# One wide product for both parts of the moving operand in the paired up-projection of a two-layer decoder

## The chip, the cores and the metric

The kernel runs on one core of a Trainium2 chip. The metric is the device time of one execution in microseconds, shown as the median of the runs. The profiled execution is a run of its own; its span (first to last instruction) is a little shorter than its time.

## The reference, cut to what matters

Two layers over 512 tokens of width 1024. Each layer has a mixing half (attention and retention from one joint projection, then gates and an output projection) and an MLP. The change is in the MLP alone:

```python
    h2 = rmsnorm(x, g_mlp)
    x = x + jnp.square(jax.nn.relu(h2 @ w_up)) @ w_down      # w_up 1024 x 4096, w_down 4096 x 1024
```

## The kernel before, in words

**Precision.** Everything is float32, but TensorE gets float32r, which keeps fewer bits. So each operand is split into a high part (a rounded copy, written by ACT) and a low part (the rest, a subtraction on DVE). A product of two such operands is three products of TensorE: high by high, high by low, low by high. The helper `products` (L276) issues them at L282, L283 and L284: weights `ah`/`al`, moving operand `bh`/`bl`.

**Weights.** They stream in 1024-column units (`raw`), in the fixed order of `unit_order`. `unit` (L243) hands out the next unit and has `split_until` (L218) split the units up to two ahead: high part on ACT (L237), low part on DVE (L238), into tiles `hi` and `lo` of a pool of three. Within these tiles the weights may begin `ASIDE` = 48 elements (192 bytes) in. With it their address lies 192 bytes from that of the moving operand, counted modulo 512; without it the distance is none.

**The MLP.** Hidden rows come in chunks of 128. The first four chunks are plain products of 512 columns (`group`). The other 28 pairs of chunks (14 a layer) use a scheme of Winograd's kind: w_up's contraction of 1024 is cut in two halves, the 512 tokens in two halves of H = 256, and a pair of chunks is computed with seven half products in place of eight. The price is sums and differences: of the moving operand once a layer (`sum_input`, L981, eight forms in tiles `by_form`), and of the weights for each pair (`add_part`, L204: L208, L211, L215, L216 on DVE). One half product is a call of `multiply` in `pair` (L1025): four k-steps, each three products of 256 columns. `block` (L1002) gives the k-steps of the input itself (tiles `xh`, `xl`), `form` (L999) those of the sums.

In `pair`, three PSUM banks (the first 256 columns of each) collect the results, in this order of the source:

```text
a  = block(0,0)              L1039  ACT copies a into b
e  = form(0)                 L1041  ACT copies e to eu
b += form(1)                 L1044  ACT copies b to eu
a += block(1,0)              L1046  DVE: z from a, relu and rstd
b += form(2)                 L1049  DVE: z from b + eu
e += block(1,1)              L1051  DVE: z from e + eu
b += form(3)                 L1055  DVE: relu and rstd of two quarters
                             L1056  DVE: z from b, relu and rstd
```

Then ACT squares z (L1059), and z is split into high and low (`split`: L289 on ACT, L290 on DVE) for w_down. w_down's products run in `two_chunks` (L344), with 512 columns, 48 for two output chunks; L1066 adds them to x. `mlp_sequence` alternates: two pairs first, then two chunks of w_down with the hidden rows of one quarter, then a pair of the next quarter, and so on. At the end of each quarter w_down needs the pair just made.

**Order.** The source's order is not the order of the queues: the framework's scheduler places each engine's instructions when the program is built, and takes w_down's products in between where a pair's operands are not ready by its reckoning. In the queue of TensorE, form(3) of a regular pair follows some 22 products of w_down. Each engine works its own queue in order and waits on semaphores. The DMAs of weights are issued on SP.

Of the kernel before, what the change touches and what calls it, by code (L numbers as in the profile page):

```python
# [11 lines left out]
F32R = mybir.dt.float32r  # L12
AF = mybir.ActivationFunctionType
# [102 lines left out]
def decoder(ctx, tc, xT, x_first, w_in, w_a, w_b, w_out, w_up, w_down, tables, decay, band, out):  # L116
# [29 lines left out]
    sink = little_x[:, P - n_gain - n_sink : P - n_gain]  # L146
    eps, half, nsink = (little_x[:, a : a + n] for a, n in ((0, 1), (8, N_KV), (16, n_sink)))
    x = little_x[:, P:].rearrange("p (k t) -> p k t", t=T)
    xh = const.tile([P, KD, T], F32R, name="xh")
    xl = const.tile([P, KD, T], F32R, name="xl")  # L150
    slots = Slots([const.tile([P, 4, T], F32R, name=f"r{i}") for i in range(9)])
    spill = dram.tile([P, KD, T], F32, name="spill")

# [64 lines left out]
    def split_until(n):  # L218
        while state["split"] < min(n, len(order)):
            i = state["split"]  # L220
            load_until(i + 3)
            paired = order[i][1] == "pair"
            if paired:
                add_part(i)
            raw = raws[i]
            if homes and i >= len(order) - len(homes):
                home = homes[len(order) - 1 - i]
                hi, lo = (home[:, 2 * a : 2 * a + 2, :].rearrange("p a t -> p (a t)") for a in range(2))
            else:

                first = ASIDE if paired or i >= len(order) - 8 else 0
                hi, lo = (wpool.tile([P, UNIT + P], F32R, tag=n, name=n)[:, first : first + UNIT] for n in ("hi", "lo"))
            for at in (LEFT,) if paired and order[i][3] == 3 else halves(i):
                if i == 0 and at.start == 0:
                    nc.vector.tensor_copy(hi[:, at], raw[:, at])
                else:
                    nc.scalar.activation(hi[:, at], raw[:, at], AF.Copy)  # L237
                nc.vector.tensor_tensor(lo[:, at], raw[:, at], f32(hi[:, at]), ALU.subtract)  # L238
            raws.pop(i - 3 if paired else i, None)
            parts[i] = (hi, lo)  # L240
            state["split"] += 1
# [240 lines left out]
    def layer_body(layer):  # L482
# [493 lines left out]

        H = T // 2
        sums = [slots.four() for _ in range(4)]
        by_form = [t[0].rearrange("p a (b t) -> p (a b) t", t=H) for t in sums]

        def sum_input(ks):  # L981

            b = [big("xg") for _ in range(2)]
            for i in range(2):
                for part, g in ((0, ks + i), (1, ks + i + 4)):
                    col = g_mlp * KD + g
                    nc.scalar.activation(b[part][:, i, :], x[:, g, :], AF.Copy, scale=gain[:, col : col + 1])
# [3 lines left out]
            hi, lo = by_form[ks // 2], by_form[2 + ks // 2]  # L991
            nc.vector.tensor_tensor(t1, b12, b11, ALU.subtract)
            nc.vector.tensor_tensor(t2, b22, t1, ALU.subtract)
            split(hi[:, 0:4, :], lo[:, 0:4, :], f[0])
            nc.vector.tensor_tensor(t3, b22, b12, ALU.subtract)
            nc.vector.tensor_tensor(t4, b21, t2, ALU.subtract)
            split(hi[:, 4:8, :], lo[:, 4:8, :], f[1])

        def form(j):  # L999
            return [tuple(by_form[2 * i + k // 2][:, 2 * j + k % 2, :] for i in range(2)) for k in range(4)]  # L1000

        def block(half, tokens):  # L1002
            at = slice(tokens * H, tokens * H + H)
            return [(xh[:, k, at], xl[:, k, at]) for k in range(4 * half, 4 * half + 4)]

        up = [[] for _ in range(4)]
        up_slots = [[] for _ in range(4)]
# [16 lines left out]

        def pair(q):  # L1025
            def multiply(ps, weights, left, moving, start=True):
                hi, lo = weights
                cols = [slice((0 if left else 4 * P) + k * P, (0 if left else 4 * P) + (k + 1) * P) for k in range(4)]
                products(ps, [((hi[:, c], lo[:, c]), m) for c, m in zip(cols, moving)], start, True, not start)

            a, e, b = (bank(ps_mm, "mm")[:, :H] for _ in range(3))
            eu, z = temp("eu"), big("z")
            part = unit("pair", layer)
            multiply(a, part, True, block(0, 0))
            nc.scalar.activation(b, a, AF.Copy)  # L1039
            multiply(e, part, False, form(0))  # L1040
            nc.scalar.activation(eu[:, :H], e, AF.Copy)  # L1041
            part = unit("pair", layer)
            multiply(b, part, True, form(1), False)
            nc.scalar.activation(eu[:, H:], b, AF.Copy)  # L1044
            multiply(a, part, False, block(1, 0), False)
            nc.vector.scalar_tensor_tensor(z[:, 0, :H], a, 0.0, rms_mlp.value[:, :H], ALU.max, ALU.mult)  # L1046
            part = unit("pair", layer)
            multiply(b, part, True, form(2), False)
            nc.vector.tensor_tensor(z[:, 1, H:], b, eu[:, :H], ALU.add)  # L1049
            multiply(e, part, False, block(1, 1), False)  # L1050
            nc.vector.tensor_tensor(z[:, 0, H:], e, eu[:, H:], ALU.add)  # L1051
# [204 lines left out]
```

## Time and profile before

| | |
|---|---|
| Median of 3 runs (lowest to highest) | 1505.5 us (1505.16 to 1505.73) |
| Profiled execution: time, span | 1504.93 us, 1503.1 us |
| Granted clock of TensorE in it | 0.998 |
| DMA, mean | 103 GB/s |
| Starts of L1039, five regular pairs | 487.1, 507.9, 528.7, 548.1, 570.2 us |
| L237, split of 1024 on ACT, mean of one | 1058 ns |
| L238, split of 1024 on DVE, mean of one | 1221 ns |

An instruction's mean duration is not what it costs its engine: products overlap on TensorE. In the lists, "idle before" is idle time of the engine just before the instructions of a group, with what ended most of it.

### The profile page before, as it was taken

How to read it: one execution, taken by the hardware profiler on the slowest of the kernel's cores; microseconds unless marked ns; L12 is line 12 of the kernel's file. 1: busy time of each engine (PE TensorE's matmuls, PEld its weight loads, DVE VectorE, ACT ScalarE, POOL GpSimd, SP SyncE). 2: the span in 40 equal slices, each digit the busy share in tenths (PEclk: the TensorE clock that was granted, in tenths of full speed). 3: DMA queues.
4: the chain of work that ended last, by engine and by line, in shares of the span. 5: the costliest groups of instructions: out<-in, count | busy, mean ns of one | idle time of the engine just before them, and what ended most of it. 6: DMA issues, size and time to landing. Idle time of an engine off the chain costs nothing.

```text
span 1503.1 us, 20508 instructions
## 1 busy us (share of the span) xinstructions
PE 1491.8 (99%) x8082; PEld 1296.0 (86%) x8082; DVE 1026.7 (68%) x1598; ACT 738.8 (49%) x1163; POOL 2.9 (0%) x13
## 2 busy tenths in 40 slices
PE   9999999999999999999999999999999999999997
PEld 7888888888888999989888888888888999899997
DVE  7877568754787666676678865777449866666664
ACT  6657355532564444444455742555326544444452
POOL 0000000000000000000000000000000000000000
PEclk9999999999999999999999999999999999999999
DMA  6422222234223233233442222222342232232331
GB/s 221 133 85 71 98 84 92 70 126 126 99 75 108 99 113 99 98 100 124 160 130 92 85 85 98 80 83 84 127 126 96 87 99 99 99 112 99 102 109 56
DMA packets 52640, 155.10 MB, mean 103 GB/s; under 512 B 6208, under 2 KB 8384, under 8 KB 52544
## 3 DMA queue, kind: packets, MB, share of 16 engines
q1 hardware_dynamic: 52400, 153.54, 31.1%
q8 instruction: 63, 1.03, 0.3%
q14 instruction: 33, 0.27, 0.1%
q10 hardware_dynamic: 144, 0.26, 0.1%
HBM read 146.96 MB, written 4.19 MB: 101 GB/s over the span
## 4 chain that ended last, share of the span: by engine, by line
PE 99%; ACT 1%; DVE 0%; issue 0%; DVEq 0%
PE mm L284 29%; PE mm L282 29%; PE mm L283 29%; PE rv L282 2%; PE rv L284 2%; PE rv L283 2%; PE score L653 1%; PE pT L618 1%; PE r L284 1%; PE r L283 1%; PE r L282 1%; PE pv L638 0%; PE pv L639 0%; PE ssq L376 0%; PE ret L283 0%; PE ret L284 0%
## 5 line engine op out<-in xcount | busy, mean ns | idle before, releaser
L237 ACT ACTIVATE hi<-raw 128x1024 fp32r<-128x1024 f32 (+1 forms) x313 | 314.7, 1013 | 504.0 <-PE mm L283 413.8
L238 DVE TENSOR_TENSOR lo<-raw,hi 128x1024 fp32r<-128x1024 f32 (+1 forms) x314 | 362.4, 1163 | 157.1 <-ACT hi L237 156.3
L283 PE MATMUL mm<-r,hi 128*128 128x512 f32 (+1 forms) x1136 | 390.2, 344 | 0.0
L282 PE MATMUL mm<-r,hi 128*128 128x512 f32 (+1 forms) x1136 | 387.7, 345 | 1.1 <-ACT mm L1039 1.1
L284 PE MATMUL mm<-r,lo 128*128 128x512 f32 (+1 forms) x1136 | 386.6, 344 | 0.0
L282 PE MATMUL mm<-xh,hi 128*128 128x512 f32 (+1 forms) x1008 | 356.4, 355 | 0.0
L283 PE MATMUL mm<-xl,hi 128*128 128x512 f32 (+1 forms) x1008 | 355.4, 354 | 0.0
L284 PE MATMUL mm<-xh,lo 128*128 128x512 f32 (+1 forms) x1008 | 354.7, 354 | 0.0
L282 PEld LDWEIGHTS mm<-r,hi 128*128 128x128 f32 x1136 | 212.5, 187 | 27.5 <-ACT mm L1039 1.5
L283 PEld LDWEIGHTS mm<-r,hi 128*128 128x128 f32 x1136 | 213.3, 188 | 26.0
L284 PEld LDWEIGHTS mm<-r,lo 128*128 128x128 f32 x1136 | 213.1, 188 | 25.6
L283 PEld LDWEIGHTS mm<-xl,hi 128*128 128x128 f32 x1008 | 189.5, 188 | 25.3
L282 PEld LDWEIGHTS mm<-xh,hi 128*128 128x128 f32 x1008 | 189.1, 188 | 25.7 <-ACT xh L292 0.5
L284 PEld LDWEIGHTS mm<-xh,lo 128*128 128x128 f32 x1008 | 189.3, 188 | 25.1
L1066 DVE TENSOR_TENSOR x<-x,mm 128x512 f32<-128x512 f32 x56 | 37.8, 686 | 33.7 <-PE mm L284 33.7
L284 PE MATMUL rv<-hi,xl 128*128 128x512 f32 x128 | 49.8, 389 | 0.0
L283 PE MATMUL rv<-lo,xh 128*128 128x512 f32 x128 | 49.8, 389 | 0.0
L282 PE MATMUL rv<-hi,xh 128*128 128x512 f32 x128 | 49.8, 390 | 0.0
L283 PE MATMUL mm<-ulo,hi 128*128 128x512 f32 (+1 forms) x128 | 46.1, 362 | 0.0
L282 PE MATMUL mm<-uhi,hi 128*128 128x512 f32 (+1 forms) x128 | 46.1, 362 | 0.0
L284 PE MATMUL mm<-uhi,lo 128*128 128x512 f32 (+1 forms) x128 | 45.5, 363 | 0.0
L1046 DVE SCALAR_TENSOR_TENSOR z<-mm,rstd 128x256 f32<-128x256 f32 x28 | 11.9, 425 | 40.2 <-PE mm L284 40.2
(188 smaller groups left out, 1683.3 us busy)
## 6 DMA issues: line engine op xcount, KB each, us to landing
raw<-w_in_in SPq DMA_DIRECT2D x89, 512.0 KB, 3.4
raw<-w_down_in SPq DMA_DIRECT2D x64, 512.0 KB, 3.3
raw<-w_up_in SPq DMA_DIRECT2D x36, 512.0 KB, 3.3
raw<-w_up_in SPq DMA_DIRECT2D x56, 256.0 KB, 2.7
raw<-w_b_in SPq DMA_DIRECT2D x16, 512.0 KB, 3.3
raw<-w_out_in SPq DMA_DIRECT2D x16, 512.0 KB, 4.0
raw<-w_a_in SPq DMA_DIRECT2D x8, 512.0 KB, 3.3
x<-xT_in SPq DMA_DIRECT2D x15, 256.0 KB, 3.8
```

What stands on the lines that cost most here:

```text
L237: nc.scalar.activation(hi[:, at], raw[:, at], AF.Copy)
L238: nc.vector.tensor_tensor(lo[:, at], raw[:, at], f32(hi[:, at]), ALU.subtract)
L282: nc.tensor.matmul(ps, ah, bh, start=start and i == 0, stop=False, **more)
L283: nc.tensor.matmul(ps, ah, bl, start=False, stop=False, **more)
L284: nc.tensor.matmul(ps, al, bh, start=False, stop=stop and i == n - 1, **more)
L618: nc.tensor.transpose(pt[:, i * P : (i + 1) * P], sm[:, at : at + P], ident)
L653: nc.tensor.matmul(ps[:, g * w : (g + 1) * w], q_s[g][:, c, at], part[:, keys], start=i == 0, stop=i == 1)
L1046: nc.vector.scalar_tensor_tensor(z[:, 0, :H], a, 0.0, rms_mlp.value[:, :H], ALU.max, ALU.mult)
L1066: nc.vector.tensor_tensor(x[:, c, :], x[:, c, :], ps, ALU.add)
```

## The change

High weights now meet both parts of the moving operand in one product. The moving operand is laid out so that its high and low parts of 256 columns can be given as one operand of 512: `xh` and `xl` become two halves of one tile `xhl`, and the sums' forms are stored with the two parts of each form side by side. The product writes a whole bank: high by high in the left half, high by low in the right half. The low weights meet the high part alone and add to the left half. So a k-step is a product of 512 and one of 256 in place of three of 256, and the halves of a bank must be added when it is read: by `join` (a copy of the right half on ACT, an add on DVE) or, where a copied bank is added as well, by `join_copied` (three adds on DVE). The copies of banks are of 512 columns. The weights of the pairs begin at 0 in their tiles in place of `ASIDE`. Relu and rstd of the first token half are taken together, like those of the second.

```diff
-    xh = const.tile([P, KD, T], F32R, name="xh")
-    xl = const.tile([P, KD, T], F32R, name="xl")
+    xhl = const.tile([P, 2, KD, T], F32R, name="xhl")
+    xh, xl = xhl[:, 0], xhl[:, 1]
...
-                first = ASIDE if paired or i >= len(order) - 8 else 0
-                hi, lo = (wpool.tile([P, UNIT + P], F32R, tag=n, name=n)[:, first : first + UNIT] for n in ("hi", "lo"))
+                first = (0, 0) if paired else (ASIDE, ASIDE) if i >= len(order) - 8 else (0, 0)
+                hi, lo = (
+                    wpool.tile([P, UNIT + P], F32R, tag=n, name=n)[:, a : a + UNIT] for n, a in zip(("hi", "lo"), first)
+                )
...
-        by_form = [t[0].rearrange("p a (b t) -> p (a b) t", t=H) for t in sums]
+        by_form = [
+            t[0].rearrange("p a (b t) -> p (a b) t", t=H).rearrange("p (j k s) t -> p j k s t", k=2, s=2) for t in sums
+        ]
...
-            split(hi[:, 0:4, :], lo[:, 0:4, :], f[0])
+            split(*parts_of_forms(ks, 0), f[0].rearrange("p (j k) t -> p j k t", k=2))
...
-            return [tuple(by_form[2 * i + k // 2][:, 2 * j + k % 2, :] for i in range(2)) for k in range(4)]
+            return [by_form[2 * (j // 2) + k // 2][:, j % 2, k % 2, :, :] for k in range(4)]
...
-            return [(xh[:, k, at], xl[:, k, at]) for k in range(4 * half, 4 * half + 4)]
+            return [xhl[:, :, k, at] for k in range(4 * half, 4 * half + 4)]
...
                 hi, lo = weights
-                cols = [slice((0 if left else 4 * P) + k * P, (0 if left else 4 * P) + (k + 1) * P) for k in range(4)]
-                products(ps, [((hi[:, c], lo[:, c]), m) for c, m in zip(cols, moving)], start, True, not start)
-            a, e, b = (bank(ps_mm, "mm")[:, :H] for _ in range(3))
-            eu, z = temp("eu"), big("z")
+                more = {} if start else {"skip_group_check": True}
+                both = ps.rearrange("p (s t) -> p s t", t=H)
+                for k, m in enumerate(moving):
+                    c = slice((0 if left else 4 * P) + k * P, (0 if left else 4 * P) + (k + 1) * P)
+                    nc.tensor.matmul(both, hi[:, c], m, start=start and k == 0, stop=False, **more)
+                    nc.tensor.matmul(ps[:, :H], lo[:, c], m[:, 0, :], start=False, stop=k == 3 and start, **more)
+
+            def join(dest, ps):
+                side = temp("side")[:, :H]
+                nc.scalar.activation(side, ps[:, H:], AF.Copy)
+                nc.vector.tensor_tensor(dest, ps[:, :H], side, ALU.add)
+
+            def join_copied(dest, ps, u):
+                nc.vector.tensor_tensor(u[:, :H], u[:, :H], u[:, H:], ALU.add)
+                nc.vector.tensor_tensor(u[:, :H], u[:, :H], ps[:, H:], ALU.add)
+                nc.vector.tensor_tensor(dest, ps[:, :H], u[:, :H], ALU.add)
+
+            a, e, b = (bank(ps_mm, "mm") for _ in range(3))
+            eu, bu, z = temp("eu"), temp("bu"), big("z")
...
-            nc.scalar.activation(eu[:, :H], e, AF.Copy)
+            nc.scalar.activation(eu, e, AF.Copy)
...
-            nc.scalar.activation(eu[:, H:], b, AF.Copy)
+            nc.scalar.activation(bu, b, AF.Copy)
             multiply(a, part, False, block(1, 0), False)
-            nc.vector.scalar_tensor_tensor(z[:, 0, :H], a, 0.0, rms_mlp.value[:, :H], ALU.max, ALU.mult)
+            join(z[:, 0, :H], a)
...
-            nc.vector.tensor_tensor(z[:, 1, H:], b, eu[:, :H], ALU.add)
+            join_copied(z[:, 1, H:], b, eu)
             multiply(e, part, False, block(1, 1), False)
-            nc.vector.tensor_tensor(z[:, 0, H:], e, eu[:, H:], ALU.add)
+            join_copied(z[:, 0, H:], e, bu)
...
-            later = rms_mlp.value[:, H:].unsqueeze(1).broadcast_to([P, 2, H])
-            nc.vector.scalar_tensor_tensor(z[:, :, H:], z[:, :, H:], 0.0, later, ALU.max, ALU.mult)
-            nc.vector.scalar_tensor_tensor(z[:, 1, :H], b, 0.0, rms_mlp.value[:, :H], ALU.max, ALU.mult)
+            for half in (1, 0):
+                at = slice(half * H, half * H + H)
+                if half == 0:
+                    join(z[:, 1, at], b)
+                factor = rms_mlp.value[:, at].unsqueeze(1).broadcast_to([P, 2, H])
+                nc.vector.scalar_tensor_tensor(z[:, :, at], z[:, :, at], 0.0, factor, ALU.max, ALU.mult)
```

More of the change, by code (lines that the diff above doesn't have):

```diff
@@ L978, in layer_body, with parts_of_forms @@
         sums = [slots.four() for _ in range(4)]
-        by_form = [t[0].rearrange("p a (b t) -> p (a b) t", t=H) for t in sums]
+        by_form = [
+            t[0].rearrange("p a (b t) -> p (a b) t", t=H).rearrange("p (j k s) t -> p j k s t", k=2, s=2) for t in sums
+        ]
+        def parts_of_forms(ks, j):
+            t = by_form[2 * (j // 2) + ks // 2]
+            return [t[:, :, :, s, :] for s in range(2)]
         def sum_input(ks):
@@ L990, in sum_input @@
             t1, t2, t3, t4 = f[0][:, 0:2, :], f[0][:, 2:4, :], f[1][:, 0:2, :], f[1][:, 2:4, :]
-            hi, lo = by_form[ks // 2], by_form[2 + ks // 2]
             nc.vector.tensor_tensor(t1, b12, b11, ALU.subtract)
             nc.vector.tensor_tensor(t2, b22, t1, ALU.subtract)
-            split(hi[:, 0:4, :], lo[:, 0:4, :], f[0])
+            split(*parts_of_forms(ks, 0), f[0].rearrange("p (j k) t -> p j k t", k=2))
             nc.vector.tensor_tensor(t3, b22, b12, ALU.subtract)
             nc.vector.tensor_tensor(t4, b21, t2, ALU.subtract)
-            split(hi[:, 4:8, :], lo[:, 4:8, :], f[1])
+            split(*parts_of_forms(ks, 2), f[1].rearrange("p (j k) t -> p j k t", k=2))
         def form(j):
-            return [tuple(by_form[2 * i + k // 2][:, 2 * j + k % 2, :] for i in range(2)) for k in range(4)]
+            return [by_form[2 * (j // 2) + k // 2][:, j % 2, k % 2, :, :] for k in range(4)]
         def block(half, tokens):
             at = slice(tokens * H, tokens * H + H)
-            return [(xh[:, k, at], xl[:, k, at]) for k in range(4 * half, 4 * half + 4)]
+            return [xhl[:, :, k, at] for k in range(4 * half, 4 * half + 4)]
         up = [[] for _ in range(4)]
```

## The prediction, made before the changed kernel ran

> **What bounds the kernel now.** I read the page first: busy shares, then the chain that ended last.
>
> ```profile
> PE 1491.8 (99%) x8082; PEld 1296.0 (86%) x8082; DVE 1026.7 (68%) x1598; ACT 738.8 (49%) x1163; POOL 2.9 (0%) x13
> ...
> PE 99%; ACT 1%; DVE 0%; issue 0%; DVEq 0%
> ```
>
> TensorE is busy for 99% of the span, and the chain back from the last instruction is 99% TensorE. So only two things move the end: how long the stream of products is, and how long TensorE stands still inside it. Work on DVE and ACT costs nothing until TensorE waits for it. Next come the groups with shapes kept apart, for the sizes of the pieces (busy us, mean ns of one, idle before).
>
> ```profile
> L282 PE MATMUL mm<-r,hi 128*128 128x256 f32 x464 | 129.8, 280 | 1.1 <-ACT mm L1039 1.1
> ...
> L1049 DVE TENSOR_TENSOR z<-mm,eu 128x256 f32<-128x256 f32 x28 | 11.9, 424 | 7.5 <-PE mm L284 7.5
> L1051 DVE TENSOR_TENSOR z<-mm,eu 128x256 f32<-128x256 f32 x28 | 11.7, 417 | 0.0
> ...
> L1039 ACT ACTIVATE mm<-mm 128x256 f32<-128x256 f32 x28 | 10.3, 368 | 28.7 <-PE mm L284 28.7
> ...
> L824 ACT ACTIVATE rr<-r 128x512 f32<-128x512 f32 x16 | 9.6, 601 | 12.9 <-PE r L284 12.8
> ```
>
> The only wait of TensorE inside the pairs is 1.1 us in all, for the copy at L1039. A product's mean of 280 ns is not its cost, since products overlap; the cost is the step from start to start. That is read in the timeline (start in us, duration, engine, line).
>
> ```profile
> 524.71 0.39 PE L283 MATMUL mm<-r,hi 128*128 128x512 f32 x1
> ...
> 527.65 0.39 PE L284 MATMUL mm<-r,lo 128*128 128x512 f32 x1
> 527.88 0.28 PE L282 MATMUL mm<-xh,hi 128*128 128x256 f32 x1
> ...
> 529.49 0.37 ACT L1039 ACTIVATE mm<-mm 128x256 f32<-128x256 f32 x1 [0.58 <-PE mm L284]
> ...
> 531.18 0.28 PE L283 MATMUL mm<-r,hi 128*128 128x256 f32 x1
> ```
>
> From 524.71 to 527.88 there are 14 steps of 512 columns: 3.17/14 = 226.4 ns. From 527.88 to 531.18 there are 28 steps of 256 columns: 3.30/28 = 117.9 ns. Half of 226.4 is 113.2, so a short product costs 4.7 ns more than its columns. Last, the windows: the first two pairs of each layer, and a regular period of one pair with its two chunks of w_down (columns: us, PE, PEld, DVE, ACT, POOL busy).
>
> ```profile
> 437.00:452.00 15.00, 14.52 (x122) 14.52 (x123) 12.12 (x19) 10.48 (x19) 0.00 (x0) 1.00 0.32 106
> 507.90:528.70 20.80, 20.80 (x134) 18.91 (x133) 14.06 (x20) 9.28 (x14) 0.00 (x0) 1.00 0.27 86
> 1180.00:1195.00 15.00, 15.00 (x129) 15.00 (x128) 12.62 (x19) 9.51 (x17) 0.00 (x0) 1.00 0.32 107
> ```
>
> DVE has 32% to spare in a regular period, but only 2.4 to 2.9 us of 15 at the two first pairs.
>
> **The stream of products.** 28 pairs run seven calls of multiply of four k-steps: 784 k-steps. Each was three products of 256 columns, 3 x 117.9 = 353.7 ns. It becomes one of 512 (high weights by both parts) and one of 256 (low weights by the high part). The 768 columns stay; a product and a weight load go. The 512 I take at 226.4; where a 512 is followed by a 256, at the entry of the pairs, the unrounded starts also give 225 to 226. The 256 is now always followed by a 512. That occurs where a pair hands over to w_down, and there the step is 115 ns, the same at all five places between 520 and 556 us. Those short weights still lay 192 bytes aside, though the weights loaded during the step lay at no distance, as they will now. In the last stage, where weights already lie at no distance, the short step is 120 (1464.78 to 1466.94: 18 steps, 2.16 us). I take 116, near to the row with the same follower. New k-step: 342.4; saving 11.3 x 784 = 8.9 us. Ends: the short one at its bare columns (113.2), 14.1 x 784 = 11.1 us; or 231, the step of the retention's 512 products before shorter ones, plus 120, which leaves 2.7 x 784 = 2.1 us. For 336 of the long products the moving operand is two runs of 256 columns lying 16 KB apart. The only product of several runs here is L262, 427 ns at a granted clock of half: 213 at full, so no sign of a cost. I take none; the 5 ns of 231 against 226 would be 1.7 us and is inside the ends.
>
> By the Trainium skill (TensorE: Matmul & The Clock Gate, "Back-to-back issue gap") a warm product alone costs its columns at 2.4 GHz plus about 2.5 ns. By that a k-step would go from 327.5 to 325.0 ns, and the whole change of the stream would be 2.0 us. The trace has 117.9 and 226.4 in place of 109.2 and 215.8, so here the measurement decides; what a stream that saves next to nothing would give is the second rival, priced from rows.
>
> **What is added on DVE and ACT.** Per pair DVE had 0.425 + 0.424 + 0.417 + 0.691 + 0.424 = 2.38 us (L1046, L1049, L1051, L1055, L1056; L1055, the 0.691, is of 512 columns). It gets two joins (one add each), two joins of copied banks (three adds each) and two products with rstd of 512: 8 x 0.42 + 2 x 0.69 = 4.74, so 2.36 us more, 66 us in all. ACT's three copies grow from 256 to 512 columns, 0.37 to 0.60 (L824 is such a copy), and two copies of 256 come: 1.44 us more, 40 us in all. In a regular period DVE goes to 16.4 and ACT to 10.7 of 20.5 us. Neither becomes the bound; the price lies in what TensorE awaits. The other edits (one tile for both parts, the forms' new order in memory, the splits written in strides) change no count and no size; I cost them at nothing, as the eight strided splits of 1024 run while w_up's first group keeps TensorE for tens of us. If that cover went, a strided write at half speed would cost some 1.2 us each, about 10 in all. No DMA is added or moved.
>
> **The waits, in the order of a pair.** (1) Bank b is copied from a while e is multiplied. In the lines above the copy ends at 529.86, and form(1) starts at 527.88 + 24 x 0.1179 = 530.71: 0.85 us of cover. The copy takes 0.23 longer and the cover is 0.05 shorter: 0.57 stays. Cost nothing. (2) The copy of b (L1044) must end before form(2) adds to b. Two multiplies stood between; the trace's ends and starts give 2.2 us of slack. In eight of the 28 pairs the new order of instructions has, on ACT, the copy of e, a split of 1024, one of 512 and then the copy of b, while TensorE has form(1), block(1,0) and one product. Behind the end of e: 0.2 + 0.60 + 1.06 + 0.63 + 0.60 = 3.09 us against 1.37 + 1.37 + 0.23 = 2.97. With a semaphore that is about 0.15 us late, eight times: 1.2 us. The low weights of that unit come next and find DVE free within the following product. (3) DVE now reads bank b twice before form(3). Form(3) stands behind 24 or so products of w_down, 5 us later, and the trace's slack there is 4.4 us, so a split of 1.22 ahead of the joins is covered. (4) In six pairs (where a quarter of the hidden rows ends) only 10 to 12 products of w_down lie between form(3) and the next pair, and ACT has the squares ahead of the next copy of b. From the end of form(3): side copy 0.2 + 0.38, behind a split on ACT about 0.5; join 0.42, rstd 0.69, two squares 1.24, copy 0.60, behind a split on DVE about 1: 5.0. Cover: 10 to 12 x 0.2264 + 2 x 1.37 = 5.0 to 5.5. So 0 to 0.5 each; I take 0.25, 1.5 us. (5) The first two pairs of a layer: DVE's 12.1 to 12.6 of 15 us grow by 2 x 2.36 to about 17. The 2 us too much can be worked off in the next period, and the low weights of w_down are ready some 0.6 to 1.3 us ahead there. I take 0.65 a layer, 1.3 us.
>
> Sum: 1.2 + 1.5 + 1.3 = 4.0 us of new waits. Ends: none, if each cover holds; 0.45 us in each of the 28 pairs, 12.6 us, if DVE's queue sets the pace (below). A gain on the waits is excluded: only 1.1 us of wait is there to be gained.
>
> Net: -8.9 + 4.0 = -4.9 us. The profiled execution took 1504.93 us (span 1503.1 and 1.8 around it), so 1500.0; the median of the runs is 0.6 above it, 1505.5, so 1500.6.
>
> **Rivals.** *The joins set the pace (slower).* Each adds three dependent steps on DVE, in a queue where a split of 1.22 us may stand ahead and where the next splits and additions of weights stand behind. L1051 with 0.0 idle before it shows that this queue is at times already full when the join comes. If the weights' low parts slip by 0.45 us a pair, 12.6 us of waits against 8.9 saved: 1509.2. It decides from 8.9/28 = 0.32 us a pair. For it: 84% busy at the first pairs before anything is added. Against: 32% to spare in the other 24 pairs, and slacks of 2 to 4 us.
>
> *The stream saves little.* Weights at no distance from the moving operand could slow both products of a k-step; the steps go to 231 and 120: 2.1 us saved, 4.0 lost: 1507.4; with waits of 2 it is no change at all. For it: the 120 of the last stage. Against: 115 where the follower is the same.
>
> *Every cover holds.* 1505.5 - 8.9 = 1496.6. For it: the order was laid out anew around the longer copies. Against: the sum of (2).
>
> That the change doesn't do what it says can be left aside: the built kernel has 784 products fewer, as counted.
>
> **How the numbers follow.** A measurement of this kernel can tell about 0.2%, 3 us, from no change. Forecast (net between -7 and 0): 0.36, of which 0.08 within 3 us. Joins: 0.27, slower. Little saved: 0.20, of which 0.15 within 3 us and 0.05 slower. Covers hold: 0.17, faster. So faster 0.28 + 0.17 = 0.45, the same 0.23, slower 0.32. The range goes from 1496.0 (all covers, saving of 9.5) up into the joins' case to 0.42 us a pair, 1508.5. Cases of both signs hold much of the chance; the forecast's own range is 1498.5 to 1505.5.
>
> **What would show it.** Right: in the pairs, steps near 226 and 116 by turns, PE at 7298 products; the copy into bank b 0.60 us; waits of TensorE in the list near 4 us in all, most for ACT (copy of b, copy into b) and for the low weights at the first pairs. Wrong: steps of 231 and 120 (second rival), or PE's idle time above 9 us with DVE as the releaser (first), or steps above 340 ns for the block operands alone, which would be the two runs.

## The result, and the profile after

The changed kernel takes 1510.55 us (median of 6 runs, 1510.31 to 1510.72) against 1505.39 us for the kernel before (6 runs beside them, 1505.16 to 1505.73). The ratio is 1.0035, with a 95% interval of 1.0025 to 1.0045: slower by 5.2 us, where 4.9 less was forecast. The span of the profiled execution is 1508.7 us, at a granted clock of 0.998; before it was 1503.1. So 5.6 us of span are to be found.

The page after, busy shares and chain:

```profile
PE 1493.6 (99%) x7298; PEld 1258.2 (83%) x7298; DVE 1077.5 (71%) x1738; ACT 763.0 (51%) x1219; POOL 2.9 (0%) x13
...
PE 97%; ACT 1%; DMA 1%; DVE 1%; issue 0%; DVEq 0%
```

784 products are gone, as the change says, and TensorE is still busy 99% of a longer span. The share of TensorE in the chain fell from 99 to 97%: some waits are new. The timeline of TensorE through a whole regular pair shows what the stream became (start in us, duration, engine, line):

```profile
529.64 0.39 PE L1041 MATMUL mm<-xhl,hi 128*128 128x512 f32 x1
529.87 0.28 PE L1042 MATMUL mm<-xhl,lo 128*128 128x256 f32 x1
529.98 0.40 PE L1041 MATMUL mm<-xhl,hi 128*128 128x512 f32 x1
...
538.09 0.39 PE L284 MATMUL mm<-r,hi 128*128 128x512 f32 x1
...
540.84 0.39 PE L284 MATMUL mm<-uhi,hi 128*128 128x512 f32 x1
...
543.56 0.39 PE L1041 MATMUL mm<-r,hi 128*128 128x512 f32 x1
```

The first k-step is the one that was forecast: 529.64 to 529.98, 0.34 us. It is the only one in this pair. From 529.64 to 538.09 there are 24 k-steps in 8.45 us, 352 ns each, where 353.7 was the step before and 342.4 the forecast. In the unrounded starts the long step has a median of 235 ns and the short one 117. Behind the pair the 12 products of w_down up to 540.84 take 2.75 us, 229 ns each, and the next 12 take 2.72, which is 226.7 again. So products of 512 columns are slow after short ones, and stay so for several products.

The list of TensorE's waits (us in total, times, longest):

```profile
PE mm L284 <- ACT hi L239: 2.1, 2, 1.0
PE mm L1041 <- ACT mm L1065: 1.6, 2, 0.8
PE warm L264 <- DVE ones L259: 1.1, 1, 1.1
PE mm L284 <- DVE x L430: 0.6, 1, 0.6
PE ssq L443 <- ACT sq L435: 0.5, 1, 0.5
PE mm L285 <- DVE r L292: 0.5, 1, 0.5
```

The first line is new, the second grew by 0.5, and the fourth and sixth are new and lie in the last stage (up to 1465.86 and 1461.97 us). The first is best seen across engines, in the timeline at the first two pairs of layer 0 (the brackets give idle time before, and its releaser):

```profile
449.06 0.63 ACT L239 ACTIVATE hi<-raw 128x512 fp32r<-128x512 f32 x1 [1.91 <-PE mm L1041]
...
450.45 1.06 ACT L239 ACTIVATE hi<-raw 128x1024 fp32r<-128x1024 f32 x1 [0.75 <-PE mm L1041]
...
451.56 0.50 PE L284 MATMUL mm<-r,hi 128*128 128x512 f32 x1 [1.03 <-ACT hi L239]
451.67 0.59 ACT L1067 ACTIVATE eu<-mm 128x512 f32<-128x512 f32 x1
...
452.15 0.60 ACT L1070 ACTIVATE bu<-mm 128x512 f32<-128x512 f32 x1
```

TensorE stands from 450.5 to 451.56 for the split of w_down's first unit. That split could not start before 450.45, since a tile of the weight pool came free only with the product that TensorE had just done. And ACT's copies of e and b of the second pair (L1067, L1070) stand behind it in ACT's queue. Before, the same copies stood ahead of that split:

```profile
448.39 0.36 ACT L1041 ACTIVATE eu<-mm 128x256 f32<-128x256 f32 x1
...
449.40 0.39 ACT L1044 ACTIVATE eu<-mm 128x256 f32<-128x256 f32 x1
450.46 1.06 ACT L237 ACTIVATE hi<-raw 128x1024 fp32r<-128x1024 f32 x1 [0.67 <-PE mm L283]
```

The windows that were shown of before, in the kernel after:

```profile
437.00:452.00 15.00, 13.45 (x74) 11.21 (x74) 11.06 (x19) 9.25 (x15) 0.00 (x0) 1.00 0.27 77
507.90:528.70 20.80, 20.80 (x105) 17.60 (x105) 15.80 (x24) 10.13 (x17) 0.00 (x0) 1.00 0.34 101
1180.00:1195.00 15.00, 13.86 (x78) 11.41 (x76) 11.73 (x19) 9.25 (x16) 0.00 (x0) 1.00 0.24 70
```

At the first pairs DVE is less busy than before (11.06 against 12.12 us), not more: nothing there is full. The engines wait for each other.

**Where 5.6 us went.** All starts of successive products were compared: where they lie more than 25 ns over 227 ns (512 columns) or 118 ns (256), the excess is counted as a wait. Waits go from 10.8 to 17.0 us, 6.2 more: 2.4 in layer 0's MLP and 4.0 in layer 1's, of which some 1.7 in the last stage. What is left, -0.6, is the stream: a k-step of 351.5 in place of 353.5 gives back 1.5 us over 784, and w_down's product goes from 227.05 to 227.73 ns on average, which over some 1340 takes 0.9. (The parts add up to 6.4; the start of the kernel gave 0.2 back.)

### The profile page after: what moved, and what is told of

It reads as the page before. It is cut to its first block, busy times and chain, and to the rows that moved or that the text cites. A ratio compares the mean times of both kernels' runs of the same rounds, so it can differ in the third digit from the quotient of the medians.

```text
span 1508.7 us, 19211 instructions
## 1 busy us (share of the span) xinstructions
PE 1493.6 (99%) x7298; PEld 1258.2 (83%) x7298; DVE 1077.5 (71%) x1738; ACT 763.0 (51%) x1219; POOL 2.9 (0%) x13
## 4 chain that ended last, share of the span: by engine, by line
PE 97%; ACT 1%; DMA 1%; DVE 1%; issue 0%; DVEq 0%
PE mm L284 22%; PE mm L285 22%; PE mm L286 22%; PE mm L1041 12%; PE mm L1042 6%; PE rv L284 2%; PE rv L286 2%; PE rv L285 2%; PE score L655 1%; PE pT L620 1%; PE r L285 1%; PE r L286 1%; PE r L284 1%; DMA raw<-w_down_in 1%; PE pv L640 0%; PE pv L641 0%
## 5 line engine op out<-in xcount | busy, mean ns | idle before, releaser
L239 ACT ACTIVATE hi<-raw 128x1024 fp32r<-128x1024 f32 (+1 forms) x313 | 315.6, 1013 | 453.4 <-PE mm L285 261.2
L284 PE MATMUL mm<-r,hi 128*128 128x512 f32 (+1 forms) x688 | 264.2, 388 | 2.1 <-ACT hi L239 2.1
L285 PE MATMUL mm<-r,hi 128*128 128x512 f32 (+1 forms) x688 | 266.2, 387 | 0.0
L284 PE MATMUL mm<-xhl,hi 128*128 128x512 f32 x672 | 262.7, 393 | 0.1
L286 PE MATMUL mm<-r,lo 128*128 128x512 f32 (+1 forms) x688 | 262.3, 387 | 0.0
L285 PE MATMUL mm<-xhl,hi 128*128 128x512 f32 x672 | 261.6, 392 | 0.0
L286 PE MATMUL mm<-xhl,lo 128*128 128x512 f32 x672 | 260.5, 392 | 0.0
L1041 PE MATMUL mm<-r,hi 128*128 128x512 f32 x448 | 162.5, 398 | 1.6 <-ACT mm L1065 1.6
L284 PEld LDWEIGHTS mm<-r,hi 128*128 128x128 f32 x688 | 128.7, 188 | 28.8 <-ACT hi L239 2.7
L285 PEld LDWEIGHTS mm<-r,hi 128*128 128x128 f32 x688 | 129.2, 188 | 25.2
L286 PEld LDWEIGHTS mm<-xhl,lo 128*128 128x128 f32 x672 | 126.3, 188 | 25.0
L284 PEld LDWEIGHTS mm<-xhl,hi 128*128 128x128 f32 x672 | 126.2, 188 | 24.9 <-ACT xhl L294 0.6
L285 PEld LDWEIGHTS mm<-xhl,hi 128*128 128x128 f32 x672 | 126.3, 188 | 24.2
L1042 PE MATMUL mm<-r,lo 128*128 128x256 f32 x448 | 125.9, 281 | 0.0
L1041 PE MATMUL mm<-xhl,hi 128*128 128x512 f32 x336 | 121.8, 397 | 0.1
L1041 PEld LDWEIGHTS mm<-r,hi 128*128 128x128 f32 x448 | 84.1, 188 | 22.4 <-ACT mm L1065 3.2
L1042 PE MATMUL mm<-xhl,lo 128*128 128x256 f32 x336 | 94.2, 280 | 0.0
L1041 PEld LDWEIGHTS mm<-xhl,hi 128*128 128x128 f32 x336 | 63.1, 188 | 15.1 <-ACT eu L1067 0.9
L1042 PEld LDWEIGHTS mm<-xhl,lo 128*128 128x128 f32 x336 | 63.4, 189 | 1.8
```

What stands on the lines that cost most here:

```text
L284: nc.tensor.matmul(ps, ah, bh, start=start and i == 0, stop=False, **more)
L285: nc.tensor.matmul(ps, ah, bl, start=False, stop=False, **more)
L286: nc.tensor.matmul(ps, al, bh, start=False, stop=stop and i == n - 1, **more)
L1041: nc.tensor.matmul(both, hi[:, c], m, start=start and k == 0, stop=False, **more)
L1042: nc.tensor.matmul(ps[:, :H], lo[:, c], m[:, 0, :], start=False, stop=k == 3 and start, **more)
```

## The experiments

Times are medians; ratios are to the kernel before, run beside it on the same chip (its medians lay between 1505.0 and 1505.5 us). Edits are against the changed kernel where nothing else is said.

**The places of the weights.** Three runs move where the pairs' weights begin.

```diff
-  first = (0, 0) if paired else ...
+  first = (0, ASIDE) if paired else ...        # e1
+  first = (ASIDE, ASIDE) if paired else ...    # e2
```

> The changed kernel with one edit: the low weights of the pairs begin 192 bytes aside, the high ones at 0. In the changed kernel a k-step of the pairs takes 235 ns (long) and 117 ns (short) in the median, 352 in all, where 342 was forecast. Theory 'place': the long product is slowed because the low weights, loaded while it runs, lie at no distance from its moving operand. Then long 226, short 115, k-step 341: 784 x 11 ns = 8.6 us less, about 1502 us. Rival 'lengths': products of 512 and 256 by turns are slow wherever the weights lie. Then the k-step stays at 352 and the time at 1510.5 us.

> The changed kernel with high and low weights of the pairs 192 bytes aside, as before the change. 'Place': long 226, but the short one, during which the next high weights are loaded, goes to 118 as in the kernel before: k-step 344, 6.3 us less, about 1504.3 us. 'Lengths': k-step 352, 1510.5 us.

e4 is the kernel before with its pairs' weights at no distance:

```diff
-  first = ASIDE if paired or i >= len(order) - 8 else 0
+  first = ASIDE if i >= len(order) - 8 else 0
```

> The kernel before with one edit: the weights of the pairs begin at 0 in their tiles. No product changes its length. 'Place': the steps of 256 go from 118 to 120 ns, as in the last stage: 2352 x 2 ns = 4.7 us more, about 1510.1 us. 'Lengths' alone says nothing of this kernel: 1505.4 us.

e1: 1509.32 (ratio 1.0027, 1.0017 to 1.0038), k-step 350.5. e2: 1509.55 (1.0030, 1.0018 to 1.0042), long 230.9 and short 118.9, k-step 349.8. e4: 1510.93 (1.0038, 1.0023 to 1.0053), the step of 256 columns 120 in place of 118; 2352 such steps by 2 ns are 4.7 of the 5.9 us measured. So the place matters to the old stream too, but neither e1 nor e2 moves the k-step of the new one below 349 or the time by more than 1.2 us.

**The stream without the joins.** e3 has the new products, but reads the banks as before: the left halves only, copies of 256 columns, no joins (the product of high weights by low parts is left out of the result).

```diff
-  nc.scalar.activation(eu, e, AF.Copy)
+  nc.scalar.activation(eu[:, :H], e[:, :H], AF.Copy)
...
-  join_copied(z[:, 1, H:], b, eu)
+  nc.vector.tensor_tensor(z[:, 1, H:], b[:, :H], eu[:, :H], ALU.add)
```

> The changed kernel without the joins: banks are read as in the kernel before, left halves only, and two of the three copies are of 256 columns again, so the high-by-low parts of the products are left out of the result. The stream of products is that of the changed kernel. Theory 'joins': the 6.2 us of waits that TensorE has more than before come from the joins' work on DVE and ACT; they go, and what is left is the stream's saving of some 1.3 us: about 1504.2 us. Rival 'order': they come from the new order of instructions and the longer copy into b, and at least half stays: 1507 us or more.

Measured: 1505.80 (1.0005, 0.9996 to 1.0014), not to be told from the kernel before. Its steps are the changed kernel's (236 and 117), its waits 11.7 us in all by the count above, and the waits for L239 and in the last stage are gone:

```profile
PE mm L1041 <- ACT mm L1065: 1.6, 2, 0.8
PE warm L264 <- DVE ones L259: 1.1, 1, 1.1
PE ssq L443 <- ACT sq L435: 0.5, 1, 0.5
```

So two things are settled at once. The stream by itself brings nothing: 784 products fewer, and no time. And the slowdown of 5 us comes with the joins, or with the copies of 512 columns of e and b, which e3 takes back with them.

**Does the turn of long and short cost it?** e5 issues a half product's four long products first and then the four short ones.

```diff
-  for k, m in enumerate(moving):
-      nc.tensor.matmul(both, hi[:, c], m, ...)
-      nc.tensor.matmul(ps[:, :H], lo[:, c], m[:, 0, :], ...)
+  for k, m in enumerate(moving):
+      nc.tensor.matmul(both, hi[:, cols[k]], m, ...)
+  for k, m in enumerate(moving):
+      nc.tensor.matmul(ps[:, :H], lo[:, cols[k]], m[:, 0, :], ...)
```

> The changed kernel with one edit: within a half product the four long products (512 columns) come first, then the four short ones (256), in place of by turns. Theory 'turns': the steps of 232 to 241 come from the turns, in which each step leaves the next one's weight load late; entries of a chain take 226 and 113. Then long 226.5, and short after short at no distance 120: 1386 ns a half product in place of 1410, 196 x 24 ns = 4.7 us less, about 1505.8 us. Rival 'long': the long product of the pairs is slow by itself (two halves of a bank, the layout of its operand): long stays at 233 or more and the time at 1510.5.

Measured: 1511.58 (1.0041, 1.0025 to 1.0056). Its timeline (groups of four in one row):

```profile
529.34 1.07 PE L1041 MATMUL mm<-xhl,hi 128*128 128x512 f32 x4
530.25 0.64 PE L1043 MATMUL mm<-xhl,lo 128*128 128x256 f32 x4
530.72 1.09 PE L1041 MATMUL mm<-r,hi 128*128 128x512 f32 x4
531.65 0.63 PE L1043 MATMUL mm<-r,lo 128*128 128x256 f32 x4
```

The four long ones at the entry, after w_down's, take 0.91 us (228 each). The four after four short ones take 0.93 (unrounded: 233, 236, 228 and 233, or 235, 233, 236 and 224 in most half products). So it isn't the single turn: long products that come after short ones are slow for several products, whatever their grouping, and two turns in a half product in place of eight save nothing.

**Where the waits come from.** e8 puts the first two pairs of each layer back to three narrow products and their old reads, with the weights 192 bytes aside.

```diff
-  pair(q)
+  pair(q, (q, i) in ((0, 2), (0, 3)))     # narrow: products of 256 columns, banks read without joins
```

> The changed kernel with the first two pairs of each layer done the old way: three products of 256, no joins, weights 192 bytes aside. The other 24 pairs are as changed. Theory 'crowd': the waits that came at the first pairs (some 2.1 us a layer beyond those of before) are the joins' work on a DVE that is already full there. They go: 4.2 us less, about 1506.3 us. Rival 'moved': the first pairs that are joined, wherever they stand, make TensorE wait, and the waits move to the next pair: 1509 us or more.

Measured: 1506.92 (1.0013, 1.0004 to 1.0023), 3.6 us less than the changed kernel; the waits at the first pairs are gone, those of the last stage remain. e12 asks whether the joins' work by itself crowds DVE and ACT: the kernel before with its three products and, in the reads, as many DVE and ACT operations as the joins make (dummy operations that don't change the values).

```diff
+  def join_copied(dest, ps, u):
+      nc.vector.tensor_tensor(u, u, u, ALU.max)
+      nc.vector.tensor_tensor(u, u, ps, ALU.add)
+      nc.vector.tensor_tensor(dest, u, u, ALU.max)
...
-  nc.vector.tensor_tensor(z[:, 1, H:], b, eu[:, :H], ALU.add)
+  join_copied(z[:, 1, H:], b, eu[:, :H])
```

> The kernel before with the joins' work and without the long products: each pair has the changed kernel's two side copies on ACT and its ten operations on DVE in the same chain, but on the left halves, with maxima of a value with itself in place of sums, so that the result stays as it was. Theory 'joins': this alone brings the waits of the changed kernel, at the first two pairs of each layer and in the last stage: 4 to 6 us more than before, 1509 to 1511 us. Rival 'order': the waits need the copies of 512 columns or the order that the long products brought; then at most 2 us more.

Measured: 1506.66 (1.0009, 1.0000 to 1.0019). DVE is as busy as in the changed kernel (1072.5 against 1077.5 us), yet no wait appears at the first pairs, and one of 0.3 in the last stage. In its queues ACT's copies stand ahead of the split, and no product of w_down stands among those of the second pair. So the joins' operations alone are not the cause. What is left is the copies of 512 columns, which e12 doesn't have (ACT is busy for 744.1 us in it, 763.0 in the changed kernel), and an order: but which? On TensorE, two products of w_down now stood ahead of 16 products of the second pair. e14 puts them behind:

```diff
+  for mm in before_last if (q, i) == (0, 0) else ():     # last products of form(2) and block(1,1)
+      behind.enter_context(tc.issue_after(mm))
   two_chunks("w_down", layer, up[q], [...])
```

> The changed kernel with one thing altered: in the first pair of each layer w_down's products of the first two chunks may be queued on TensorE only after the second pair's products that are ready by then (its form step and its second block product). Order theory (the waits at the first two pairs come from two w_down products queued ahead of 16 ready products): the wait of 1.19 us at 449 us and most of the three that follow it (0.11, 0.20, 0.11) go in each layer, about 1.5 us twice, so about 1507.5 us against 1510.5 for the changed kernel. Rival (VectorE and ScalarE are full there, whatever the order): the same waits come back a few products later, on the split of the weights or on the copies out, and the time stays at 1509.5 or above.

Measured: 1513.64 (1.0052, 1.0038 to 1.0066), slower still. The theory of TensorE's order alone fell, and the timeline says why:

```profile
450.91 1.06 ACT L239 ACTIVATE hi<-raw 128x1024 fp32r<-128x1024 f32 x1 [0.76 <-PE mm L1042]
...
452.14 0.59 ACT L1069 ACTIVATE eu<-mm 128x512 f32<-128x512 f32 x1
...
452.78 0.50 PE L1042 MATMUL mm<-xhl,hi 128*128 128x512 f32 x1 [1.79 <-ACT eu L1069]
```

The 16 products weren't ready at all. block(1,1) adds to e, which ACT must have copied first, and that copy stands behind the split that waits for TensorE. e16 takes this away as well. The split of w_down's first unit, and the last join of the first pair with what follows it, are issued behind the second pair's copy of b, which brings ACT's queue into the order of before:

```diff
   last_copy.append(nc.scalar.activation(bu, b, AF.Copy).ins)
+  while held:                                  # the first pair's reads of form(3) and what follows
+      with tc.issue_after(last_copy[-1]):
+          held.pop()()
...
+  if order[i][1] == "w_down" and [o[1] for o in order[i - 8 : i]] == ["pair"] * 8:
+      behind.enter_context(tc.issue_after(last_copy[-1]))    # around the high part's split on ACT
```

> The order of before as to the first two pairs, for the changed kernel: on TensorE w_down's first products stand behind the ready products of the second pair (as in the run before this one), and on ScalarE the copies of e and b of the second pair stand ahead of the split of w_down's first unit, which waits for a buffer that TensorE gives back only at 450.4 us; the last join of the first pair is issued behind these copies. Nothing else is changed, places and joins least of all. Theory 'ScalarE's queue' (what TensorE awaits at 450 us stands behind a split that awaits TensorE): the waits of 1.19 + 0.11 + 0.20 + 0.11 us go in both layers, 3.2 us, about 1507.3 us. Rival (VectorE and ScalarE have too much to do there): waits of over 1 us come up again within some 24 products, on a split or on low weights: 1509.5 or more.

Measured: 1508.05 (1.0018, 1.0008 to 1.0027), 2.5 us less than the changed kernel. Its timeline of ACT, and its waits:

```profile
447.97 0.58 ACT L1076 ACTIVATE eu<-mm 128x512 f32<-128x512 f32 x1
448.88 0.60 ACT L1079 ACTIVATE bu<-mm 128x512 f32<-128x512 f32 x1 [0.33 <-PE mm L1050]
449.87 0.63 ACT L244 ACTIVATE hi<-raw 128x512 fp32r<-128x512 f32 x1 [0.39 <-PE mm L1049]
451.25 1.06 ACT L244 ACTIVATE hi<-raw 128x1024 fp32r<-128x1024 f32 x1 [0.76 <-PE mm L1049]
```

```profile
PE mm L1049 <- ACT mm L1074: 1.6, 2, 0.8
PE warm L269 <- DVE ones L264: 1.1, 1, 1.1
PE ssq L448 <- ACT sq L440: 0.5, 1, 0.5
PE mm L290 <- DVE r L297: 0.5, 1, 0.5
PE mm L289 <- DVE x L435: 0.3, 1, 0.3
```

The split still starts only when TensorE gives the tile back (451.25), but now both copies are done by then and TensorE has ready products. The wait for it is gone from both layers, with all joins and all copies of 512 columns in place: for this wait, 3.2 of the 6.2 us, the order of ACT's queue, together with TensorE's, was the cause. Which of the moves on ACT is needed, and whether ACT's order would do without TensorE's, no run shows. The gain is 0.7 less than expected; waits in all are 14.6 us against 17.0. The trace has one new wait in each layer, 0.37 us at 474.6 and 1217.4, where w_down's high weights come late from ACT. The kernel is still 2.7 us slower than before.

**A stream that does gain.** e6 keeps the first two pairs and the last pair of each layer narrow and issues long products first elsewhere, low weights 192 bytes aside. e10 takes turns instead, with both weights 96 bytes aside.

```diff
+  pair(q, (q, i) in ((0, 2), (0, 3), (3, 3)))
+  first = ... (0, ASIDE) if paired ...        # e6
+  first = ... (24, 24) if paired ...          # e10
```

> The long products first, low weights 192 bytes aside, and the first two and the last pair of each layer the old way. If the steps are 226.5 and 118 (short after short, 192 bytes aside) and the waits stay near those of the kernel before, 22 pairs save 616 x 9.2 ns = 5.7 us: about 1499.5 us, faster than both kernels. If the joins make TensorE wait elsewhere, or long products stay at 233, 1503 us or more.

> The changed kernel with long and short by turns, the weights of the pairs 96 bytes aside (347.1 ns a k-step in the sweep of places), and the first two pairs and the last pair of each layer the old way. 616 k-steps save 6.6 ns each against 353.7, 4.1 us; some 1.1 us is given back where the products of w_down start after a short one (two or more slow steps), and the waits stay within 0.3 us of those before: about 1502.4 us, faster than both kernels. If the places of the sweep do not hold in a whole run, or the joins of the other pairs make TensorE wait, 1505 us or more.

e6: 1507.21 (1.0013, 1.0005 to 1.0022). Its long products take 241, 238, 233 and 231 ns in most half products that don't follow w_down, and w_down's first nine behind a pair are slow, 61 ns in all. e10: 1503.36 (0.9987, 0.9978 to 0.9996), k-step 347.4, with only the waits of before: the first version that beats the kernel before. e6 missed its 1499.5 by 7.7 us, since its long products stayed slow; e10 missed its 1502.4 by 1.0.

Two runs, each of one execution, swept the places, 32 bytes further in each of a layer's 14 pairs. The first held the high weights at 0 in layer 0, the second at 96 bytes.

> The changed kernel with another place of the weights in each pair: pair p of 14 has its low weights 32 x p bytes aside in layer 0 (high at 0), and both 32 x p bytes aside in layer 1. Read from the steps, not from the time. 'Place': some place has the k-step at 342 (226 and 116), and the k-step goes up and down with the place. 'Turns': no place comes below about 347, the best that a pair of the changed kernel had.

> A second sweep of places, read from the steps: in layer 0 the high weights lie 96 bytes aside and the low ones of pair p 32 x p; in layer 1 the low ones 96 and the high ones 32 x p. If only the weights loaded during the long product count (the low ones), layer 1 is flat and layer 0 goes up and down; if the place of both against each other counts, both go up and down, with the best where both are 96 (347 ns). Below 345 ns anywhere would say that a better place was missed.

They took 1509.98 and 1509.96. Mean k-step (ns) in layer 0, by the low weights' place in bytes; the columns 0 and 32 are the two first pairs:

```text
low weights    0     32    64    96    128   160   192   224   256   288   320   352   384   416
high at 0    352.2 349.2 347.6 349.8 350.3 351.9 351.3 350.1 351.2 349.3 347.2 349.8 350.3 351.9
high at 96   348.4 351.6 353.1 347.1 351.0 352.5 348.2 346.8 347.0 343.9 351.6 347.1 351.0 352.4
```

With the high weights at 0 the row repeats after 256 bytes to within 1 ns. At 96 the places from 96 to 160 repeat to 0.1 ns, and the first three differ from those 256 bytes further by 1.4, 7.7 and 1.5; two of these are the first pairs, where half products of two pairs alternate.

A column is one pair, though, and pairs differ by themselves. In the changed kernel, with all weights at 0, they run from 347.5 to 352.5, and there too the fourth to sixth pairs agree with the twelfth to fourteenth. So this table alone shows neither what a single place is worth nor a period of 256 bytes; what a place is worth is read from whole runs. In layer 1 of the second run, where the low weights stayed at 96 bytes and the high ones moved, the k-step went from 347.1 to 353.1, so the low weights' place is not all that counts. e15 takes the best place, 96 and 288, into e10:

```diff
-  else (24, 24) if paired
+  else (24, 72) if paired
```

> The hybrid by turns (first two pairs and the last pair of each layer as before, the others as changed), with the high weights 96 bytes and the low weights 288 bytes aside in place of 96 and 96. Place theory (the second sweep's best row, 343.9 ns a step against 347.4 at 96 and 96, holds for all pairs): 616 steps in changed pairs by 3.2 to 3.5 ns is 2.0 to 2.2 us less than the hybrid's 1503.4, so about 1501.3, below both kernels. Rival (the row of the sweep was one pair's own state, not its place): steps stay near 347 and the time near 1503.4.

Measured: 1501.60 (0.9976, 0.9966 to 0.9986), faster than both kernels: 3.8 us less than before. Its k-steps have a mean of 344.9. In the timeline of one pair:

```profile
527.50 0.40 PE L1045 MATMUL mm<-xhl,hi 128*128 128x512 f32 x1
...
533.00 0.40 PE L1045 MATMUL mm<-xhl,hi 128*128 128x512 f32 x1
533.24 0.39 PE L1045 MATMUL mm<-r,hi 128*128 128x512 f32 x1
...
535.83 0.39 PE L284 MATMUL mm<-r,hi 128*128 128x512 f32 x1
```

The first 16 k-steps take 5.50 us, 343.8 ns each, close to the 342.4 that was forecast for no distance. From 533.00 on, where two long products follow each other because two half products overlap, the last eight take 2.83 us, 354 each: in this pair the gain holds while long and short take turns without a break.

Last, e17 puts the place of e15 into e16: all 28 pairs wide, orders and places mended.

> The run before with the places of the pairs' weights 96 bytes (high) and 288 bytes (low) aside in place of none: the change in all 28 pairs, with its order and its places mended. If both effects hold at their sizes, 784 steps by (351.5 - 344.9) = 5.2 us less than that run: about 1502.1 us, below the kernel before by 0.2%; what is left over it is the last stage, whose waits (about 1.7 us) stay. If the places bring nothing in the first two pairs and the last: about 1503.1.

Measured: 1504.39 (0.9994, 0.9985 to 1.0003), 3.7 us below e16 and 6.2 below the changed kernel, but not to be told from the kernel before. It missed 1502.1 by 2.3: e16 itself lay 0.75 above the 1507.3 assumed, the k-step is 345.9 and not 344.9 (0.8 us over 784), and w_down's product costs 228.2 and not 227.7 ns (0.7 over 1340).

## Why the prediction was wrong, by its own steps

**The stream, -8.9 us: the term that failed.** It measured about -0.6 in the traces and nothing in e3. The long step was taken at 226.4 and came at a median of 235; the short one, taken at 116, came at 117. The short step was read at the hand-over of a pair to w_down, where it is 115, and only that one step was read (at four places between 520 and 556 us and a fifth at 557). The profile before already showed the price: the two products behind it take 232 and 231 ns in place of 226.5, so what the short one saves is more than given back. The row for the long step ("where a 512 is followed by a 256") came from long products that follow long ones. Neither row had the changed stream's history. The low end of the term (231 and 120, 2.1 us saved) was the nearest to it, and it was given to the rival. Its 231, the retention's step "before shorter ones", was read from the wrong side. In the kernel before, these products of 512 come behind shorter ones as well:

```profile
266.73 0.27 PE L284 MATMUL ret<-r,r 128*128 128x128 f32 x1
266.85 0.44 PE L282 MATMUL r<-r,r 128*128 128x512 f32 x1
267.12 0.40 PE L283 MATMUL r<-r,r 128*128 128x512 f32 x1
267.36 0.39 PE L284 MATMUL r<-r,r 128*128 128x512 f32 x1
267.59 0.33 PE L282 MATMUL r<-r,r 128*128 128x384 f32 x1
```

Unrounded, the three take 280, 233 and 231 ns. At 210.75 us, where long products stand in front, the last one before the 384 takes 226. So rows of the kind that the changed stream needed, long behind short, stood in the profile before.

By the Trainium skill (TensorE: Matmul & The Clock Gate, "Back-to-back issue gap") dropping a product saves, as an estimate, about 2.5 ns a k-step, 2.0 us in all. The k-step did fall by 2.0 ns, but its products take 235 and 117 ns and not the 216 and 109 of that rule, w_down took back more than half, and by places alone the same k-step went from 352 (e16) to 345.9 (e17): no run here shows the rule to be what acts.

**The waits, +4.0 us: a size not far off, from the wrong places.** They grew by 6.2. (1) The copy into b, costed at nothing, cost 0.5 over both layers, at the entry of the MLP. (2), 1.2 us, cost nothing that the traces show. (3) was right. (4), 1.5 us, came in four pairs at 0.2 us each, 0.8 in all. These four are not in TensorE's list of waits, but the starts of products show them. In this one the copy into b stands behind the squares on ACT and ends at 633.70, and the first weight load of form(1) waits for it:

```profile
632.06 1.15 ACT L1088 ACTIVATE z<-z 128x512 f32<-128x512 f32 x2 [2.08 <-DVE z L1085]
633.12 0.58 ACT L1065 ACTIVATE mm<-mm 128x512 f32<-128x512 f32 x1
633.75 0.19 PEld L1041 LDWEIGHTS mm<-r,hi 128*128 128x128 f32 x1 [0.24 <-ACT mm L1065]
```

(5), 1.3 us, measured 3.5: 3.2 in the two stands at the first pairs, and 0.3 where low weights come late from DVE (446.5 us). It was priced as work that DVE can't finish in time, while DVE and ACT were idle there (1.12 and 0.75 us at 450 us, the one behind ACT's split, the other behind TensorE); e16 shows an order of the queues. The prediction took the changed queue's order into account only for (2); the same comparison at the first pairs would have shown the split of w_down's unit ahead of the copies of e and b. The last stage, 1.7 us, was not foreseen: there TensorE waits for the low parts of the last pair's rows (L292) and for x (L430), both on DVE. e3, e10 and e15, which have no joins in the last pair, don't show these waits.

**DVE and ACT work.** 66 and 40 us were predicted and 50.8 and 24.2 measured. The durations were right (joins 0.41 to 0.42, copies 0.58 to 0.60), but adjacent operations overlap: joins start 0.33 us after one another.

**The rivals.** "The stream saves little" (1507.4) was right in its first half, with steps of 235 and 117 in place of 231 and 120. But its mechanism held in part only: taking the weights aside (e1, e2) brings a fifth of the 5 us, and the slow long products stay at most places tried. "The joins set the pace" (1509.2) was nearest in time, but by luck: its sum was 12.6 us of waits against 8.9 saved, the runs have 6.2 against next to nothing, and half of the waits come from an order in two places and not from DVE's queue in every pair. That they add, a stream without its saving and joins with their waits, was in no case; with the stream at 0 and the waits at 4.0, the forecast's own sum would have been 1509.5. The edits costed at nothing (strided splits, operands of two runs) cost nothing: blocks, with the two runs, had a k-step of 350.7 where a long product followed, and forms 351.7.

**Still open.** Why long products are slow after short ones, and why the weights' place changes it, no run here shows. That the steps repeat in cycles ([232, 118], [241, 120], [236, 113] at no distance) is what is seen, not a cause. No run puts the copies of 512 columns into the kernel before, and none takes the joins out of the last pair alone, so the waits of the last stage are put down to its joins by e10 and e15, which change other things too.

## What to carry to other kernels

The cost of one product is not a property of its size: read it over a whole stretch that has the sequence of the new stream, and count what the following products give back, before multiplying by hundreds. Where a change lengthens a read of PSUM, compare the queues of both kernels around the tightest place, and look for an instruction that waits for the engine at the bound and has others queued behind it on which that same engine will wait. In this kernel, to save products was worth little by itself, since the columns stayed the same.

## What the runs showed of the hardware that was not expected

- Products of 512 columns behind products of 256 mostly took 228 to 241 ns in place of 226.5, for up to nine products (e6).
- The step depends on where the weights lie against the moving operand. The best of the places tried (96 and 288 bytes) gave 344.9 ns a k-step over 22 pairs, against 347.4 with both at 96 and 351.5 with no distance.
- In e14 TensorE stood still for 2.0 us at 450.8, and soon after ran at half clock for 3.4 us. Its windows (the seventh number from the left without brackets, just before the DMA share, is the granted clock):

```profile
453.00:454.00 1.00, 1.00 (x5) 0.86 (x5) 1.00 (x4) 0.48 (x2) 0.00 (x0) 0.61 0.01 4
454.00:455.00 1.00, 1.00 (x5) 0.81 (x4) 1.00 (x3) 0.00 (x0) 0.00 (x0) 0.50 0.90 156
455.00:456.00 1.00, 1.00 (x5) 0.90 (x4) 0.73 (x3) 0.81 (x2) 0.00 (x0) 0.50 0.84 322
```

The same stand in layer 1, 2.0 us at 1197, was followed by a clock of 1.00. By the Trainium skill (TensorE: Matmul & The Clock Gate, "What's actually happening") the clock drops after an idle window of about 3.4 us, and these windows run freely; here 2.0 us was enough one time of two. A wait of some 2 us can so cost nearly twice its length: in layer 0 the excess was 3.6 us. While the clock was 0.50, long and short products by turns took 427 and 213 ns, two to one like their columns, so the slow long step was not seen there.
